# Feed-forward matmuls of a float32r transformer block: both activation parts as one 512-column moving operand, and the down projection after all gates and ups

## The chip, the cores and the metric

The kernel runs on one NeuronCore of a Trainium2 chip. The metric is device time in microseconds (us) of one execution; the table below gives the median of several. TensorE (PE) does the matrix products, with weight loads shown apart as PEld; VectorE (DVE), ScalarE (ACT) and GpSimd (POOL) do the element-wise work; SyncE (SP) issues nearly all DMA transfers.

## The reference, cut to what matters

Two transformer blocks act on 256 tokens of 1024 features. Between attention, a state-space mixer and a memory attention there are four feed-forward layers, all of the same form, with 2816 hidden features:

```
hn = rmsnorm(x, gain)
x = x + f * (silu(hn @ w_gate) * (hn @ w_up)) @ w_down      # f = 1 (twice), then 0.5 (twice)
```

`w_gate` and `w_up` are 1024 x 2816 and `w_down` is 2816 x 1024, all in float32, and all weights come from HBM once.

## The kernel before, in words

**Layout.** Activations lie with features on the partitions: `xt` is [128, 8 blocks of 128 features, 256 tokens]. Each operand is kept in two parts, a rounded one (high, names ending in h, or `whi`) and what is left of it (low, names ending in l, or `wlo`), both in the type float32r. `mm3` (lines 306 to 308) makes a product of high by high, high by low and low by high, so three matmuls of 256 columns for each k-tile of 128 rows and each block of 128 output rows. The weights are the stationary operand, and each matmul has its own weight load.

**Weights.** The weights are cut on the host into slabs of [128, 2048] (1 MB). `_make` loads a slab into `raw` (two buffers, SP's queue), and cuts each half of 1024 columns: ACT rounds it to `whi` (L279), DVE subtracts to make `wlo` (L281). `whi` and `wlo` have five buffers of half a slab each, and a slab is made two slabs ahead of its use. One slab feeds 48 matmuls.

**A feed-forward layer** (`ffn`) walks over 11 chunks of 256 hidden features. A chunk has a gate slab, an up slab and a down slab. `gemm_feat` fills one PSUM bank with two blocks of 256 tokens; it uses the first half of the slab (k-tiles 0 to 3) for both blocks, then the second half. DVE scales the gate bank (L522), ACT applies Silu (L523), POOL scales once more (L524); DVE multiplies the up bank by it (L528), ACT rounds (L531) and DVE subtracts (L532), which gives the down projection's operand `hh`, `hl`. The down projection of the chunk before follows each chunk: `gemm_out` adds its two k-tiles to four PSUM banks (`acc`) that live through the whole layer. At the end `add` adds the four banks to `xt`, one after the other (L510, or L512 with the factor 0.5).

**Order.** A scheduler orders the instructions of each engine when the kernel is built, by priority and by when it takes operands to be ready; each engine then runs its list in that order. `norm` makes the next layer's operand out of `xt` (ACT L438, DVE L439, squares on ACT and POOL) at high priority; the factor of each token (`rb`) is multiplied in after the matmuls, so that the matmuls don't wait for it.

Of the kernel before, what the change touches and what calls it, by code (L numbers as in the profile page):

```python
# [52 lines left out]
def weight_plan():  # L53
# [14 lines left out]
    def ffn(kind, layer):  # L68
        for c in range(11):
            feat(f"{kind}_gate", layer, c * 256, 256)  # L70
            feat(f"{kind}_up", layer, c * 256, 256)
            if c >= 1:
                out(f"{kind}_down", layer, 2 * (c - 1), 2)
        out(f"{kind}_down", layer, 20, 2)
# [7 lines left out]
    # layer 0  # L82
# [11 lines left out]
    # layer 1  # L94
# [8 lines left out]
    # second block  # L103
# [50 lines left out]
def pack_weights(w):  # L154
# [24 lines left out]
    for s, (name, layer, kind, k0, n0) in enumerate(weight_plan()):  # L179
        nk, n = {"f": (8, 256), "t": (4, 512), "o": (2, 1024)}[kind]  # L180
        out[s].reshape(P, nk, n)[:] = rows(mats[(name, layer)], k0, nk, n0, n)
# [3 lines left out]
def pack_params(w):  # L185
# [16 lines left out]
    def states(a):  # L202
        # [32 groups, 64 states, ...] -> [(half, state), 16 groups of a half, ...]
# [19 lines left out]
# ---------------------------------------------------------------- the program  # L223
class Kernel:
# [15 lines left out]
    # -- tiles  # L240
# [15 lines left out]
    # -- weights: a slab comes in float32 and is cut into two parts of 12 bits each  # L256
    def _make(self, upto, first=None):
        nc = self.nc
        while self.made <= min(upto, len(self.plan) - 1):
# [4 lines left out]
            else:  # L264
                # the first slab comes in parts, among those of its operand
# [44 lines left out]
    def operand(self, pool=None, tag="a"):  # L310
        """Four k-tiles of a transposed activation for all tokens, in two parts."""
# [1222 lines left out]
```

## Time and profile before

| | |
|---|---|
| time, median of 3 runs | 1269.5 us (1267.67 to 1269.79) |
| profiled execution: span | 1268.1 us |
| PE busy / PEld busy | 1232.9 us (97%) / 1184.7 us (93%) |
| DVE busy / ACT busy / POOL busy | 797.9 us (63%) / 619.3 us (49%) / 211.6 us (17%) |
| matmuls | 9798 |
| HBM read | 205.57 MB, 164 GB/s over the span |

The span is that of the one profiled execution, and every duration below is from it; it lies 1.4 us under the median of the runs. A busy time is a union: matmuls overlap one another in the trace (a 256-column matmul lasts 0.28 us, the next one starts before it ends), so a matmul's price is the distance between two starts.

### The profile page before, as it was taken

The page shows a single profiled execution, that of the slowest core. Times are in us where ns is not written, and L with a number is a line of the kernel's source. Part 1 is how long each engine was busy: PE and PEld are TensorE (multiplying, and loading weights), DVE is VectorE, ACT ScalarE, POOL GpSimd, SP SyncE. Part 2 cuts the span into 40 slices and gives each one's busy share as a digit, 9 for nine tenths or more (in the row PEclk, how much of TensorE's full clock was granted, in tenths as well). Part 3 has the DMA queues.
Part 4 walks back from the last instruction along what each step waited for, and adds up shares of the span by engine and source line. Part 5 has one row for each costly group of instructions (what it writes and reads, how often), then busy time and mean ns, then how long its engine had stood idle before and what let it go on. Part 6 is the DMA issues. An engine that isn't in the chain of part 4 may idle for free.

```text
span 1268.1 us, 23060 instructions
## 1 busy us (share of the span) xinstructions
PE 1232.9 (97%) x9798; PEld 1184.7 (93%) x9798; DVE 797.9 (63%) x967; ACT 619.3 (49%) x875; POOL 211.6 (17%) x177
## 2 busy tenths in 40 slices
PE   5898999999999999999999999999999999999997
PEld 5777999999999789999999999998889999999997
DVE  8988575555576548655557555557766666655553
ACT  6553564344457656444445444446664544544343
POOL 7674030000020003000002000002301102100001
PEclk9987999999999999999999999999999999999998
DMA  6552345445553225545545545546532434545441
GB/s 208 165 169 70 125 177 199 170 168 195 199 173 133 100 91 201 178 169 195 200 169 186 181 170 197 195 172 208 201 132 101 163 107 160 204 168 198 168 170 63
DMA packets 36791, 209.12 MB, mean 165 GB/s; under 512 B 3920, under 2 KB 9808, under 8 KB 12752
## 3 DMA queue, kind: packets, MB, share of 16 engines
q1 hardware_dynamic: 35824, 205.48, 46.2%
q8 instruction: 77, 1.26, 0.4%
q0 software_dynamic: 576, 1.64, 0.4%
q10 hardware_dynamic: 288, 0.52, 0.1%
q14 instruction: 26, 0.21, 0.0%
HBM read 205.57 MB, written 2.06 MB: 164 GB/s over the span
## 4 chain that ended last, share of the span: by engine, by line
PE 88%; DVE 7%; DMA 2%; issue 1%; ACT 1%; POOL 0%; DVEq 0%; ACTq 0%; POOLq 0%
PE mm L306 15%; PE mm L307 15%; PE mm L308 15%; PE acc L308 11%; PE acc L306 11%; PE acc L307 11%; DVE wlo L281 2%; DMA raw<-in_wts 1%; PE tr L378 1%; PE acc L1166 1%; DVE al L439 1%; PE acc L601 1%; PE tr L396 1%; PE mm L567 1%; PE acc L1193 1%
## 5 line engine op out<-in xcount | busy, mean ns | idle before, releaser
L281 DVE TENSOR_TENSOR wlo<-raw,whi 128x1024 fp32r<-128x1024 f32 (+1 forms) x378 | 468.1, 1249 | 309.9 <-ACT whi L279 305.1
L279 ACT CAST whi<-raw 128x1024 fp32r<-128x1024 f32 (+1 forms) x378 | 388.4, 1042 | 421.8 <-PE acc L307 174.3
L306 PE MATMUL mm<-ah,whi 128*128 128x256 f32 x1504 | 425.8, 284 | 6.9 <-ACT whi L279 6.5
L308 PE MATMUL mm<-ah,wlo 128*128 128x256 f32 x1504 | 426.6, 284 | 0.8 <-DVE wlo L281 0.7
L307 PE MATMUL mm<-al,whi 128*128 128x256 f32 x1504 | 426.7, 284 | 0.0
L306 PEld LDWEIGHTS mm<-ah,whi 128*128 128x128 f32 x1504 | 289.0, 193 | 8.1 <-ACT whi L279 6.8
L308 PEld LDWEIGHTS mm<-ah,wlo 128*128 128x128 f32 x1504 | 289.4, 193 | 1.7 <-DVE wlo L281 1.5
L307 PEld LDWEIGHTS mm<-al,whi 128*128 128x128 f32 x1504 | 289.5, 193 | 0.6
L307 PE MATMUL acc<-hl,whi 128*128 128x256 f32 x704 | 199.3, 283 | 0.2 <-DVE hl L532 0.2
L308 PE MATMUL acc<-hh,wlo 128*128 128x256 f32 x704 | 199.1, 283 | 0.0
L306 PE MATMUL acc<-hh,whi 128*128 128x256 f32 x704 | 198.8, 283 | 0.0
L524 POOL TENSOR_TENSOR sg<-sg,rb 128x512 f32<-128x512 f32 x44 | 59.8, 1358 | 599.0 <-ACT sg L523 599.0
L307 PEld LDWEIGHTS acc<-hl,whi 128*128 128x128 f32 x704 | 135.1, 192 | 0.5 <-DVE hl L532 0.4
L308 PEld LDWEIGHTS acc<-hh,wlo 128*128 128x128 f32 x704 | 135.2, 192 | 0.0
L306 PEld LDWEIGHTS acc<-hh,whi 128*128 128x128 f32 x704 | 134.9, 192 | 0.2 <-ACT hh L531 0.2
L307 PE MATMUL acc<-al,whi 128*128 128x256 f32 x368 | 104.2, 285 | 0.0
L308 PE MATMUL acc<-ah,wlo 128*128 128x256 f32 x368 | 103.3, 284 | 0.0
L306 PE MATMUL acc<-ah,whi 128*128 128x256 f32 x368 | 102.2, 285 | 0.0
L448 POOL TENSOR_TENSOR ssq<-ssq,sq 128x512 f32<-128x512 f32 x26 | 42.4, 1629 | 275.0 <-issue 158.4
L523 ACT ACTIVATE sg<-sg 128x512 f32<-128x512 f32 x44 | 27.8, 631 | 97.8 <-DVE sg L522 97.8
L307 PEld LDWEIGHTS acc<-al,whi 128*128 128x128 f32 x368 | 70.6, 192 | 0.2
L308 PEld LDWEIGHTS acc<-ah,wlo 128*128 128x128 f32 x368 | 70.2, 192 | 0.2
(378 smaller groups left out, 1563.6 us busy)
## 6 DMA issues: line engine op xcount, KB each, us to landing
raw<-in_wts SPq DMA_DIRECT2D x187, 1024.0 KB, 4.9
raw<-in_mem SPq DMA_DIRECT2D x4, 512.0 KB, 4.7
eb<-lag SPq DMA_DIRECT2D x4, 512.0 KB, 4.7
x<-in_x SPq DMA_DIRECT2D x4, 256.0 KB, 5.1
raw<-in_wts SPq DMA_DIRECT2D x4, 256.0 KB, 5.3
sprm<-in_prm SPq DMA_DIRECT2D x1, 512.0 KB, 9.0
ud<-s SPq DMA_DIRECT2D x1, 512.0 KB, 2.6
uu<-ud SPq DMA_DIRECT2D x8, 64.0 KB, 4.4
```

The source lines that it names most:

```text
L279: nc.scalar.copy(hi[:, c:c + n], src)
L281: nc.vector.tensor_tensor(lo[:, c:c + n], src, hi[:, c:c + n].bitcast(F32), ALU.subtract)
L306: mm(out, a[0], b[0], start=start, stop=False, skip_group_check=True)
L307: mm(out, a[0], b[1], start=False, stop=False, skip_group_check=True)
L308: mm(out, a[1], b[0], start=False, stop=stop, skip_group_check=True)
L378: self.nc.tensor.transpose(out, in_, self.ident[:k, :k])
L396: nc.tensor.matmul(ps[:, t:t + 1], sq[:, t * P:(t + 1) * P], self.ones[:, 0:1], start=(i == 0 and t == 0), stop=(i == len(sqs) - 1), skip_ ...
L439: lo = nc.vector.scalar_tensor_tensor(lo, x[:, b, :], g, hi.bitcast(F32), ALU.mult, ALU.subtract).ins
L448: nc.gpsimd.tensor_tensor(ssq, ssq, q, ALU.add)
L523: nc.scalar.activation(sg, sg, AF.Silu)
L524: nc.gpsimd.tensor_tensor(sg, sg, rb2, ALU.mult)
L567: nc.tensor.matmul(scv[:, i, :], qt[r, qb, t * P:(t + 1) * P], kt[r, kblock(qb), 0:keys], start=False, stop=(i == per - 1))
```

## The change

In the feed-forward layers the high and the low part of an activation lie in one tile, one behind the other. A product with a high weight part streams both parts in one matmul of 512 columns, into a bank whose first 256 columns are the sum for the high part and whose last 256 are that for the low part; a low weight part streams the high activations alone (256 columns, added to the first 256). So a block of 128 output rows takes a whole bank, and evacuating it adds the two halves: ACT copies the second half out, DVE adds the first (in `half`), and the gate's scaling reads SBUF. All 11 chunks' gates and ups come first, and their outputs stay in 11 tiles `h0` to `h10`. Then the down projection goes by output blocks: 22 k-tiles into one bank, and two DVE operations that add its halves to `xt`. The down slabs hold 16 tiles of 128 x 128 in that order. Operands elsewhere use the same joined tile but are multiplied by `mm3` as before. An unused option of `norm` and the comments are gone.

```diff
 def ffn(kind, layer):                      # in weight_plan
         for c in range(11):
             feat(f"{kind}_gate", layer, c * 256, 256)
             feat(f"{kind}_up", layer, c * 256, 256)
-            if c >= 1:
-                out(f"{kind}_down", layer, 2 * (c - 1), 2)
-        out(f"{kind}_down", layer, 20, 2)
+        for c in range(11):
+            plan.append((f"{kind}_down", layer, "d", c * 16, 0))
...
+class Parts(tuple):
+    def __new__(cls, x):
+        self = super().__new__(cls, (x[:, 0], x[:, 1]))
+        self.both = x
+        return self
...
     def operand(self, pool=None, tag="a"):
         if pool is not None:
-            return tuple(self.t(pool, [P, 4, 256], tag + x, F32R) for x in "hl")
-        return tuple(self.t(self.ap4, [P, 4, 256], "a" + x, F32R, bufs=self.A_BUFS) for x in "hl")
+            x = self.t(pool, [P, 2, 4, 256], tag, F32R)
+        else:
+            x = self.t(self.ap4, [P, 2, 4, 256], "a", F32R, bufs=self.A_BUFS)
+        return Parts(x)
...
+    def mm2(self, out, w, x, first, last):
+        mm = self.nc.tensor.matmul
+        mm(out[:, 0, :], w[1], x[:, 0], start=first, stop=False, skip_group_check=True)
+        mm(out, w[0], x, start=False, stop=last, skip_group_check=True)
...
     def ffn(self, kind, layer, gain, factor):
...
+        def half(ps, dst):
+            v = ps.rearrange("p (i t) -> p i t", i=2)
+            y = self.t(fp, [P, 256], "half", bufs=4)
+            nc.scalar.copy(y, v[:, 1])
+            nc.vector.tensor_tensor(dst, v[:, 0], y, ALU.add)
+
+        def products(name, c, tag, evac):
+            w = self.slab(f"{kind}_{name}", layer, "f", 0, c * 256)
+            for b in range(2):
+                ps = self.ps(tag)
+                out = ps.rearrange("p (i t) -> p i t", i=2)
+                for k in range(8):
+                    self.mm2(out, w(k * 256 + b * P, P), ops[k // 4].both[:, :, k % 4, :], k == 0, k == 7)
+                evac(b, ps)
 
         for c in range(11):
             sg = self.t(fp, [P, 2, 256], "sg", bufs=2)
...
+            h = self.t(fp, [P, 2, 256], "h", bufs=2)
+            x = self.t(fp, [P, 2, 2, 256], f"h{c}", F32R)
+            hs.append(x)
+            products("gate", c, "acc", lambda b, ps, sg=sg: half(ps, sg[:, b]))
+            nc.vector.tensor_tensor(sg, sg, rb2, ALU.mult)
+            nc.scalar.activation(sg, sg, AF.Silu)
+            nc.gpsimd.tensor_tensor(sg, sg, rb2, ALU.mult)
+            products("up", c, "mm", lambda b, ps, h=h: half(ps, h[:, b]))
+            nc.vector.tensor_tensor(h, h, sg, ALU.mult)
+            nc.scalar.copy(x[:, 0], h)
+            nc.vector.tensor_tensor(x[:, 1], h, x[:, 0].bitcast(F32), ALU.subtract)
+        n = 0
+        for o in range(8):
+            ps = self.ps("acc")
+            out = ps.rearrange("p (i t) -> p i t", i=2)
+            for k in range(22):
+                if n % 16 == 0:
+                    w = self.slab(f"{kind}_down", layer, "d", n, 0, ahead=LASTF if n == 160 else None)
+                self.mm2(out, w(n % 16 * P, P), hs[k // 2][:, :, k % 2, :], k == 0, k == 21)
+                n += 1
+            with self.tc.high_priority(offset=self.HASTE):
+                y = self.t(fp, [P, 256], "y", bufs=2)
+                x = self.xt[:, o, :]
+                nc.vector.scalar_tensor_tensor(y, out[:, 0], factor, x, ALU.mult, ALU.add)
+                nc.vector.scalar_tensor_tensor(x, out[:, 1], factor, y, ALU.mult, ALU.add)
```

The first place is TensorE's list where the last feed-forward layer begins. Before, `mm` 11361 is the gate's bank and `mm` 11423 the up's; `ah`, `al` are the operand's parts.

```order
L306 MATMUL mm_11361<-ah_11307,whi_11185 128x256
L306 MATMUL mm_11423<-ah_11307,whi_11243 128x256
L307 MATMUL mm_11361<-al_11308,whi_11185 128x256
L308 MATMUL mm_11361<-ah_11307,wlo_11186 128x256
L306 MATMUL mm_11361<-ah_11307,whi_11185 128x256
L307 MATMUL mm_11423<-al_11308,whi_11243 128x256
L308 MATMUL mm_11423<-ah_11307,wlo_11244 128x256
```

In the changed kernel `a` is the joined tile; the two `acc` banks are the gate's two blocks, the two `mm` banks the up's.

```order
L366 MATMUL acc_10250<-a_10196,wlo_10075 128x256
L366 MATMUL mm_10303<-a_10196,wlo_10133 128x256
L366 MATMUL mm_10323<-a_10196,wlo_10133 128x256
L366 MATMUL acc_10270<-a_10196,wlo_10075 128x256
L367 MATMUL acc_10250<-a_10196,whi_10074 128x512
L366 MATMUL acc_10250<-a_10196,wlo_10075 128x256
L367 MATMUL acc_10270<-a_10196,whi_10074 128x512
L366 MATMUL acc_10270<-a_10196,wlo_10075 128x256
```

Three matmuls of 256 columns have become one of 256 and one of 512, a low weight part now comes first, and four blocks of gate and up are taken in turn as the k-tiles come, as before.

The second place is VectorE's list over one chunk in the middle of the gates and ups of the last layer. Before, with a down slab in the chunk:

```order
L522 TENSOR_TENSOR sg_12598<-mm_12609,rb_11348 128x512
L281 TENSOR_TENSOR wlo_12664<-raw_12661,whi_12663 128x1024
L281 TENSOR_TENSOR wlo_12668<-raw_12661,whi_12667 128x1024
L528 TENSOR_TENSOR h_12720<-mm_12671,sg_12598 128x512
L281 TENSOR_TENSOR wlo_12729<-raw_12726,whi_12728 128x1024
L532 TENSOR_TENSOR hl_12723<-h_12720,hh_12722 128x512
L281 TENSOR_TENSOR wlo_12733<-raw_12726,whi_12732 128x1024
L281 TENSOR_TENSOR wlo_12788<-raw_12785,whi_12787 128x1024
L281 TENSOR_TENSOR wlo_12792<-raw_12785,whi_12791 128x1024
```

In the changed kernel (L526 is the add of a bank's two halves, L544 the gate's scaling, L548 the product, L550 the low part):

```order
L526 TENSOR_TENSOR sg_11000<-acc_11013,half_11030 128x256
L550 TENSOR_TENSOR h_1863_10893<-h_10892,h_1863_10893 128x512
L295 TENSOR_TENSOR wlo_11010<-raw_11003,whi_11009 128x1024
L526 TENSOR_TENSOR sg_11000<-acc_11033,half_11050 128x256
L295 TENSOR_TENSOR wlo_11059<-raw_11056,whi_11058 128x1024
L544 TENSOR_TENSOR sg_11000<-sg_11000,rb_10235 128x512
L526 TENSOR_TENSOR h_11001<-mm_11066,half_11083 128x256
L295 TENSOR_TENSOR wlo_11063<-raw_11056,whi_11062 128x1024
L526 TENSOR_TENSOR h_11001<-mm_11086,half_11103 128x256
L295 TENSOR_TENSOR wlo_11115<-raw_11112,whi_11114 128x1024
L548 TENSOR_TENSOR h_11001<-h_11001,sg_11000 128x512
```

A chunk has two slabs instead of three, so four cuts instead of six, and four adds are new among them.

The third place is ScalarE's list where the last chunk's hidden features are rounded. Before, `hh` is that of the last chunk, and `ssq` is the final norm's square:

```order
L523 ACTIVATE sg_13156<-sg_13156 128x512
L279 CAST whi_13221<-raw_13219 128x1024
L279 CAST whi_13225<-raw_13219 128x1024
L531 CAST hh_13280<-h_13278 128x512
L1443 ACTIVATE ssq_13388<-x_78 128x512
```

In the changed kernel `raw` 11383 is the second down slab, `raw` 11437 the third, and L525 is the copy of a bank's second half:

```order
L545 ACTIVATE sg_11327<-sg_11327 128x512
L293 CAST whi_11389<-raw_11383 128x1024
L525 COPY half_11430<-mm_11413 128x256
L293 CAST whi_11439<-raw_11437 128x1024
L293 CAST whi_11443<-raw_11437 128x1024
L549 CAST h_1947_11329<-h_11328 128x512
L293 CAST whi_11481<-raw_11479 128x1024
```

The last chunk's rounding (L549) now stands behind both cuts of the third down slab.

## Rows read from the trace of the kernel before

**Rows 1.** The page: busy times, chain that ended last.
```profile
PE 1232.9 (97%) x9798; PEld 1184.7 (93%) x9798; DVE 797.9 (63%) x967; ACT 619.3 (49%) x875; POOL 211.6 (17%) x177
PE 88%; DVE 7%; DMA 2%; issue 1%; ACT 1%; POOL 0%; DVEq 0%; ACTq 0%; POOLq 0%
```

**Rows 2.** Windows: us; PE, PEld, DVE, ACT, POOL busy; granted clock; DMA share; GB/s.
```profile
520.00:537.28 17.28, 17.28 (x146) 17.28 (x145) 9.50 (x10) 7.25 (x8) 1.30 (x1) 1.00 0.52 184
700.00:860.00 160.00, 160.00 (x1336) 160.00 (x1335) 88.66 (x85) 66.88 (x74) 11.72 (x9) 1.00 0.52 185
```

**Rows 3.** Timeline of TensorE, feed-forward: start us, us, instruction; 20 starts from first to last.
```profile
330.00 0.28 PE L306 MATMUL acc<-hh,whi 128*128 128x256 f32 x1
...
332.40 0.28 PE L308 MATMUL acc<-hh,wlo 128*128 128x256 f32 x1
```

**Rows 4.** Timeline of TensorE, 512-column matmuls of the mixer; 18 starts from first to last.
```profile
869.82 0.39 PE L307 MATMUL acc<-wlo,ah 128*128 128x512 f32 x1
...
873.90 0.39 PE L307 MATMUL acc<-wlo,ah 128*128 128x512 f32 x1
```

**Rows 5.** Timeline of TensorE, 512 columns between 256 columns, in layer 1's attention.
```profile
412.80 0.40 PE L1193 MATMUL acc<-sph,trih 128*128 128x512 f32 x1
413.03 0.28 PE L308 MATMUL mm<-ah,wlo 128*128 128x256 f32 x1
413.15 0.28 PE L306 MATMUL mm<-ah,whi 128*128 128x256 f32 x1
...
413.39 0.40 PE L1193 MATMUL acc<-sph,trih 128*128 128x512 f32 x1
413.63 0.28 PE L308 MATMUL mm<-ah,wlo 128*128 128x256 f32 x1
```

**Rows 6.** Timeline of TensorE, a 512-column moving operand read as two rows of 256.
```profile
922.57 0.40 PE L563 MATMUL mm<-dilh,identr 128*128 128x512 f32 x1
922.80 0.40 PE L563 MATMUL mm<-dill,identr 128*128 128x512 f32 x1
```

**Rows 7.** Groups by line, 700 to 860 us: xcount, busy us, mean ns, idle before.
```profile
L281 DVE TENSOR_TENSOR wlo<-raw,whi 128x1024 fp32r<-128x1024 f32 x56 | 70.1, 1265 | 57.9 <-ACT whi L279 57.6
L279 ACT CAST whi<-raw 128x1024 fp32r<-128x1024 f32 x55 | 56.7, 1047 | 67.4 <-PE acc L307 35.8 <-PE mm L307 31.6
L524 POOL TENSOR_TENSOR sg<-sg,rb 128x512 f32<-128x512 f32 x9 | 11.7, 1302 | 142.0 <-ACT sg L523 142.0
L532 DVE TENSOR_TENSOR hl<-h,hh 128x512 fp32r<-128x512 f32 x10 | 6.8, 683 | 0.0
L528 DVE TENSOR_TENSOR h<-mm,sg 128x512 f32<-128x512 f32 x9 | 6.2, 691 | 6.3 <-PE mm L308 6.3
L531 ACT CAST hh<-h 128x512 fp32r<-128x512 f32 x10 | 6.2, 615 | 0.2 <-DVE h L528 0.2
L523 ACT ACTIVATE sg<-sg 128x512 f32<-128x512 f32 x9 | 5.7, 632 | 24.2 <-DVE sg L522 24.2
```

**Rows 8.** Timeline, single operations on 256 columns: ACT out of PSUM, DVE on SBUF.
```profile
1261.23 0.37 ACT L408 COPY rb<-tr 128x256 f32<-128x256 f32 x1 [0.79 <-PE tr L406]
483.27 0.87 DVE L439 SCALAR_TENSOR_TENSOR al<-x,prm,ah 128x256 fp32r<-128x256 f32 x2
```

**Rows 9.** Timeline, second feed-forward layer: first matmuls, last piece of its operand.
```profile
484.75 0.40 PE L306 MATMUL mm<-ah,whi 128*128 128x256 f32 x2
490.61 2.40 DVE L439 SCALAR_TENSOR_TENSOR al<-x,prm,ah 128x256 fp32r<-128x256 f32 x2
```

**Rows 10.** Timeline, end of the last feed-forward layer: last add, square, mean.
```profile
1255.84 0.69 DVE L512 SCALAR_TENSOR_TENSOR x<-acc,x 128x512 f32<-128x512 f32 x1 [0.74 <-PE acc L308]
1256.62 0.63 ACT L1443 ACTIVATE sq<-x 128x512 f32<-128x512 f32 x1 [0.86 <-DVE x L512]
1258.63 0.16 DVE L400 TENSOR_SCALAR rs<-tr 128x2 f32<-128x2 f32 x1 [2.10 <-PE tr L396]
```

**Rows 11.** Waits of SP's queue, 520 to 860 us: total us, times, longest.
```profile
SPq L263 <- DVE wlo L281: 289.9, 59, 7.9
```

More of the change, by code (lines that the diff above doesn't have):

```diff
@@ L179, in pack_weights @@
     for s, (name, layer, kind, k0, n0) in enumerate(weight_plan()):
+        if kind == "d":
+            for j in range(16):
+                o, k = divmod(k0 + j, DFF // P)
+                out[s][:, j * P:(j + 1) * P] = mats[(name, layer)][k * P:(k + 1) * P, o * P:(o + 1) * P]
+            continue
         nk, n = {"f": (8, 256), "t": (4, 512), "o": (2, 1024)}[kind]
@@ L411, in inv_rms, with norm, _norm @@
         return rb, [r[:, t:t + 1] for t in range(nt)]
-    def norm(self, x, gain, tag="rb", make=True, haste=True, pool=None, whole=False, soon=False):
+    def norm(self, x, gain, tag="rb", make=True, haste=True, pool=None, soon=False):
         if not haste:
-            return self._norm(x, gain, tag, make, pool, whole, soon)
+            return self._norm(x, gain, tag, make, pool, soon)
         with self.tc.high_priority(offset=self.HASTE):
-            return self._norm(x, gain, tag, make, pool, whole, soon)
-    def _norm(self, x, gain, tag, make, pool, whole, soon):
+            return self._norm(x, gain, tag, make, pool, soon)
+    def _norm(self, x, gain, tag, make, pool, soon):
         nc = self.nc
         ops = None
-        if whole:
-            ops = [(self.t(self.ap4, [P, 4, 256], x, bufs=self.A_BUFS),) for x in ("ah", "al")]
-        elif make:
+        if make:
             ops = [self.operand(pool, f"m{i}") for i in range(2)]
@@ L457, in _norm @@
             sqs = [ssq[:, :256]]
-        if x is self.xt and make and not whole and self.at:
+        if x is self.xt and make and self.at:
             pin, self.pin = self.pin, lo if PINN else self.pin
@@ L503, in ffn @@
         rb2 = rb.unsqueeze(1).to_broadcast([P, 2, 256])
-        acc = None
-        hts = {}
-        def add(pr, ps):
-            x = self.xt[:, 2 * pr:2 * pr + 2, :]
-            if factor == 1.0:
-                nc.vector.tensor_tensor(x, ps, x, ALU.add)
-            else:
-                nc.vector.scalar_tensor_tensor(x, ps, factor, x, ALU.mult, ALU.add)
-        def down(c, done=None):
-            w = self.slab(f"{kind}_down", layer, "o", 2 * c, 0, ahead=LASTF if c == 10 else None)
-            self.gemm_out(acc, w, [hts.pop(c)], (0, 1), c == 0, c == 10, done)
+        hs = []
@@ L518, in ffn @@
         for c in range(11):
             sg = self.t(fp, [P, 2, 256], "sg", bufs=2)
-            def gate(_, ps):
-                nc.vector.tensor_tensor(sg, ps, rb2, ALU.mult)
-                nc.scalar.activation(sg, sg, AF.Silu)
-                nc.gpsimd.tensor_tensor(sg, sg, rb2, ALU.mult)
-            def up(_, ps):
-                h = self.t(fp, [P, 2, 256], "h", bufs=2)
-                nc.vector.tensor_tensor(h, ps, sg, ALU.mult)
-                hi = self.t(fp, [P, 2, 256], "hh", F32R, bufs=2)
-                lo = self.t(fp, [P, 2, 256], "hl", F32R, bufs=2)
-                nc.scalar.copy(hi, h)
-                nc.vector.tensor_tensor(lo, h, hi.bitcast(F32), ALU.subtract)
-                hts[c] = (hi, lo)
@@ L535, in ffn @@
-            tag = "acc" if c == 1 else "mm"
-            self.gemm_feat(ops, f"{kind}_gate", layer, c * 256, 256, gate, tag)
-            self.gemm_feat(ops, f"{kind}_up", layer, c * 256, 256, up, tag)
-            if c == 1:
-                acc = [self.ps("acc") for _ in range(4)]
-            if c >= 1:
-                down(c - 1)
-        down(10, add)
+            h = self.t(fp, [P, 2, 256], "h", bufs=2)
+            x = self.t(fp, [P, 2, 2, 256], f"h{c}", F32R)
+            hs.append(x)
@@ L946, in ssm_in @@
         gts = []
-        for q in range(4):
-            gts.append(self.t(self.ap4, [P, 2, 4, 8, 16], "ah" if q % 2 == 0 else "al", F32, bufs=self.A_BUFS))
+        for q in range(2):
+            x = self.t(self.ap4, [P, 2, 2, 4, 8, 16], "a", F32, bufs=self.A_BUFS)
+            gts += [x[:, 0], x[:, 1]]
         def outs(q):
```

6 lines of the change are left out of this document (removed).

## Prediction

> **What bounds the kernel now.** I read the page first. TensorE is busy 97% of the span, and 88% of the chain that ended last is TensorE's [rows 1]; no other engine passes 63%. Then the windows: inside a feed-forward layer TensorE is busy for all of a 160 us stretch with the clock at 1.00, that is at the upper of its two levels, 2.4 GHz, while DVE is busy 55% and ACT 42% of it [rows 2]. So within these layers a change pays exactly what it takes off TensorE's stream, as long as no other engine becomes later than the stream. The third view is the timeline, because busy times of overlapping matmuls say nothing of their price: 20 starts of 256-column matmuls take 2.40 us, 120.0 ns each [rows 3]; 1336 of them in 160 us is the same number [rows 2]. A layer has 11 x 3 slabs x 48 = 1584 such matmuls, 190.1 us; the four layers take 760 us of the 1268.
>
> **What the change removes from TensorE.** For each k-tile and each block of 128 output rows, three matmuls of 256 columns (360 ns) become one of 256 and one of 512. The columns are the same, 768; a start is saved. There are 1584 / 3 = 528 such triples in a layer and 2112 in all. What the saved start is worth depends on the price of a 512-column float32r matmul:
>
> - In a long stream of them, 18 starts take 4.08 us, 226.7 ns each [rows 4]. The columns that a 512 has over a 256 cost 106.7 ns, which is 256 columns at 2.4 GHz; so both widths carry the same 13.3 ns on top of their columns, and that is what goes with the third matmul. A pair would take 120 + 226.7 = 346.7 ns: 13.3 ns saved, 2112 times, 28.1 us.
> - Where a 512 stands between 256s, which is the form that the change makes, it takes 0.23 us, and the 256 behind it 0.12 [rows 5]; in the same short stretch one takes 0.24. A moving operand read as two rows of 256, as the joined tile is, also takes 0.23 [rows 6]. With 230 ns the pair takes 350 and 10 ns are saved: 21.1 us. With 0.24 nothing is saved.
>
> The long stream settles at its price after some starts, and the new stream is as long and as regular, so I don't take the single places alone; they are nearest in form, so I don't take the stream alone either. I take the middle of 346.7 and 350, 348.4 ns: 11.6 ns x 2112 = 24.5 us. Both ends stay in the range, and 0.24 is a rival. The weight loads fall from three to two. PEld is busy through the whole stretch too [rows 2], so they could be what sets the 120 ns; but a 512 gives the next load nearly twice the time and carries the same 13.3 ns [rows 4], so I count nothing for the load that goes, and keep it as a rival.
>
> The Trainium skill ("TensorE: Matmul & The Clock Gate", Part 1 and the section on the back-to-back issue gap) says that a warm matmul starts N / 2.4 GHz plus about 2.5 ns after the one before. By that a triple would cost 3 x 2.5 ns over its columns and the pair 2 x 2.5, and the change would give 2112 x 2.5 ns = 5.3 us. The rows here have 13.3 ns in place of 2.5, at both widths, and the sum goes by the rows.
>
> **What it adds, and what hides it.** Each bank's two halves must be added: four ACT copies and four DVE adds of 256 columns for each chunk. A chunk of gate and up now takes 32 pairs, 11.15 us. ACT in it: four cuts at 1.047, Silu 0.632, the rounding 0.615 [rows 7] and four copies at 0.37 [rows 8] make 6.9 us. DVE: four cuts at 1.265, three operations on 512 columns at about 0.69 [rows 7], and four adds. An add of 256 columns out of PSUM has no row; one on SBUF costs 0.44 (two in 0.87) [rows 8], one on 512 columns out of PSUM 0.69 [rows 7]. With 0.44, nearer in size, DVE needs 8.9 us, with 0.69 9.9. Both are under 11.15, so the adds lie beside the stream. If that cover went, each us above 11.15 would cost 44 us (44 chunks). The down slabs need less: two cuts and about one add of `xt` for 5.6 us.
>
> *Weights.* A gate or up slab is now read through for its first block, then for its second, so its first half comes free at three quarters of the slab instead of at half. With five half-slab buffers the cut of the second half of the slab after next then starts at three quarters of this slab and is needed at a quarter of that one: 1.5 slabs, 8.4 us, for 2.3 us of work [rows 7]. SP's queue today waits for DVE to free `raw`, up to 7.9 us at a time [rows 11], so transfers have room; the same bytes move.
>
> *Queued behind such a wait.* The copies of a bank's half stand behind these cuts on ACT's list. A gate bank has four buffers, and an up bank's next use is 8.4 us after its end, so a cut that waits for the current slab to be used up delays nothing that TensorE needs.
>
> *Start of the down projection.* ACT rounds the last chunk behind the cuts of the third down slab (the third place shown above), and the second of these cuts waits until half of the first down slab is used: 8 pairs, 2.8 us. Then cut, DVE's subtraction of it, and the low part of the hidden features: 2.8 + 1.05 + 1.27 + 0.68 = 5.8 us [rows 7]. TensorE needs it at the 21st of 22 k-tiles, 7.0 us. The slack is 1.2 us, so I count nothing; without it this costs under 2 us a layer.
>
> *Start of a layer.* Today the last piece of the operand is ready 8.3 us after the first matmul (490.61 + 2.40 less 484.75) [rows 9], and nothing waits long because gate and up are worked on together. In the changed list the last k-tile's low part is needed after some 38 pairs' worth of work less what is put off: by the list's columns at these prices, 9.7 us. Slack 1.4 us; if it goes, some 1 to 2 us in each of four layers.
>
> *End of a layer.* The blocks of `xt` now become ready one by one, 7.7 us apart, and only the last is late. Behind the last matmul of all stand two dependent operations of 0.44 us [rows 8] instead of one add of 0.69 [rows 10], then the same square and the same sum: +0.2 us. After the other three layers the next product starts with earlier k-tiles, and only the last one or two of eight wait for this.
>
> *Elsewhere.* Operands in joined tiles give the scheduler slightly other orders in the first layer's mixer; I count zero, plus or minus 3 us.
>
> **Sum.** Span 1268.1 - 24.5 + 0.2 = 1243.8 us. The median of the runs lies 1.4 us above the span, so 1245.2. With the ends of the pair's price: 1241.6 to 1248.6.
>
> **The rivals.**
> - *Waits at the seams.* The slacks of 1.2 and 1.4 us are small, and lists are in order. For it: DVE's pieces stretch to 1.2 us when POOL adds squares beside them (2.40 for two, against 0.87) [rows 8, 9]. Against it: today's layers start with the same work. Eight seams at 1 us: 1253.
> - *A 512 costs more when it alternates.* At 235 ns the pair takes 355, and 10.6 us are left: 1259. From 240 ns on nothing is saved (1270), and each further ns costs 2.1 us. For it: the one row of 0.24 [rows 5]; against it: its neighbours and the stream [rows 4, 5, 6].
> - *DVE becomes the bound of gates and ups*, the case on the slow side as a mechanism of its own. Place: the 44 chunks. It begins at 11.15 us of DVE for each chunk and undoes the whole gain at 11.7 (44 x 0.56 = 24.5). I have 8.9 to 9.9; POOL works 1.3 us in a chunk [rows 2], and if DVE did nothing in that time it would be 11.2 at the worst. At 12 us: 1283.
> - *The third matmul gives back little*: the 13.3 ns belong to the pair of weights and not to the start, so that only some 2.5 ns go: 5.3 us, 1264. The 512's own 13.3 [rows 4] speaks against it. The rule of the Trainium skill named above would put the time here.
> - *The 256 behind a 512 is cheaper* because its weights had twice the time to load. At 110 ns the pair takes 337 with the stream's 226.7: 48 us, 1221. The row behind a 512 has 0.12 [rows 5].
> - That the change does nothing can't be: the list shows the pairs.
>
> **Chances.** Likeliest case 0.68; seams 0.13; alternating price between 351 and 360 ns 0.06; little given back 0.03; pair or DVE on the slow side 0.05; cheaper than 1241 0.05. The predicted time is that of the likeliest, 1245. The range from 1236 to 1257 leaves out the slow side, the cases near 1260 and the far end of the fast side. About 0.2% (2.5 us) is what a measurement of this kernel can tell from no change: the shown runs spread over 2.1 us. Faster 0.93, same 0.02, slower 0.05.
>
> **What would show it.** In the changed profile: starts that alternate 0.12 and 0.23 us in the feed-forward layers (right), or 0.24 and more (wrong price); the stretch of a layer down from 190 to about 184 us; no idle of TensorE put down to ACT's copies, DVE's adds or the cuts; DVE's busy share in gates and ups near 80%, in the down part near 60%; matmuls down by 2112 to some 7690. Idle in front of the first matmul on a half-ready operand, or before the last chunk's k-tiles of the first output block, would speak for the seams. The prediction is wrong if the pair does not take 346 to 351 ns, or if TensorE waits by chunks.

## The result, and the profile after

The changed kernel takes 1246.6 us (median of 4 runs, 1243.8 to 1252.7) against 1268.9 us of the kernel before; the ratio is 0.9834, with a 95% interval of 0.9807 to 0.9861. The profiled execution has a span of 1242.1 us, 26.0 us less than before. 1245 was forecast for the median and 1243.8 for the span.

The page, busy times and chain, which answer to [rows 1]:

```profile
PE 1211.7 (98%) x7686; PEld 1072.7 (86%) x7686; DVE 868.8 (70%) x1191; ACT 676.6 (54%) x1052; POOL 211.2 (17%) x177
PE 92%; DVE 5%; DMA 1%; issue 1%; ACT 1%; POOL 0%; DVEq 0%; ACTq 0%
```

TensorE still ends the chain, with a larger share than before, and 7686 matmuls are left of 9798. The windows of the second layer, once in gates and ups and once in the down projection (columns as in [rows 2]):

```profile
500.00:590.00 90.00, 90.00 (x521) 79.38 (x520) 70.25 (x96) 52.79 (x85) 11.63 (x9) 1.00 0.53 187
605.00:660.00 55.00, 55.00 (x314) 47.75 (x313) 37.34 (x45) 26.83 (x33) 2.94 (x3) 1.00 0.55 194
```

TensorE is busy for every microsecond of both, at the upper level of its clock. DVE is busy 78% of the first (80% was forecast) and 68% of the second (60%). Now the timeline of TensorE (start, us, instruction): two pairs of gates and ups, and the same place 30 pairs later; then two starts of the down projection, also 30 pairs apart.

```profile
530.13 0.28 PE L366 MATMUL mm<-a,wlo 128*128 128x256 f32 x1
530.24 0.39 PE L367 MATMUL mm<-a,whi 128*128 128x512 f32 x1
530.47 0.28 PE L366 MATMUL mm<-a,wlo 128*128 128x256 f32 x1
530.59 0.39 PE L367 MATMUL mm<-a,whi 128*128 128x512 f32 x1
...
540.53 0.28 PE L366 MATMUL acc<-a,wlo 128*128 128x256 f32 x1
...
640.21 0.28 PE L366 MATMUL acc<-h,wlo 128*128 128x256 f32 x1
640.33 0.40 PE L367 MATMUL acc<-h,whi 128*128 128x512 f32 x1
640.57 0.28 PE L366 MATMUL acc<-h,wlo 128*128 128x256 f32 x1
...
650.81 0.28 PE L366 MATMUL acc<-h,wlo 128*128 128x256 f32 x1
```

Starts alternate 0.12 and 0.23 us, as forecast. But the two stretches differ: 30 pairs take 10.40 us in gates and ups, 346.7 ns each, and 10.60 us in the down projection, 353.3 ns each. Neither is the 348.4 of the prediction. Over all pairs of the four layers the distance behind a 256-column matmul averages 117.2 ns and that behind a 512-column one 232.2, 349.4 in sum.

The two layers in the middle follow one another, so they give a clean length. They begin at 484.75 before [rows 9] and 478.81 after, and the next product begins here, before:

```profile
867.08 0.40 PE L306 MATMUL acc<-whi,ah 128*128 128x512 f32 x1
```

and here, after (the first matmul of the layers and the first one behind them):

```profile
478.81 0.28 PE L366 MATMUL acc<-a,wlo 128*128 128x256 f32 x1
...
849.80 0.39 PE L320 MATMUL acc<-whi,a 128*128 128x512 f32 x1
```

That is 382.3 us before and 371.0 after. Read the same way, all four layers take 765.3 us before and 741.2 after (185.1, 185.1, 185.9 and 185.1): 24.1 us of the 26.0. The groups of DVE and ACT in gates and ups (500 to 590 us; columns as in [rows 7]):

```profile
L295 DVE TENSOR_TENSOR wlo<-raw,whi 128x1024 fp32r<-128x1024 f32 x32 | 40.8, 1277 | 16.8 <-ACT whi L293 16.8
L293 ACT CAST whi<-raw 128x1024 fp32r<-128x1024 f32 x32 | 33.5, 1047 | 8.6 <-DMA raw<-in_wts 8.3
L546 POOL TENSOR_TENSOR sg<-sg,rb 128x512 f32<-128x512 f32 x9 | 11.6, 1296 | 78.4 <-ACT sg L545 78.4
L526 DVE TENSOR_TENSOR h<-mm,half 128x256 f32<-128x256 f32 x16 | 6.6, 413 | 0.0
L544 DVE TENSOR_TENSOR sg<-sg,rb 128x512 f32<-128x512 f32 x9 | 6.1, 684 | 0.0
L525 ACT COPY half<-acc 128x256 f32<-128x256 f32 x16 | 5.8, 364 | 0.0
```

The new add of 256 columns out of PSUM, which had no row before, takes 0.41 us and the copy 0.36. A chunk costs DVE 4 x 1.277 + 4 x 0.413 + 3 x 0.684 = 8.8 us beside 11.1 us of TensorE. The end, as [rows 10] had it:

```profile
1230.35 0.42 DVE L565 SCALAR_TENSOR_TENSOR y<-acc,x 128x256 f32<-128x256 f32 x1 [6.89 <-PE acc L367]
1230.81 0.42 DVE L566 SCALAR_TENSOR_TENSOR x<-acc,y 128x256 f32<-128x256 f32 x1
1231.33 0.63 ACT L1468 ACTIVATE sq<-x 128x512 f32<-128x512 f32 x1 [13.53 <-DVE x L566]
```

From the first operation on the last bank to the square: 0.98 us, 0.78 before.

### The profile page after: what moved, and what is told of

Its sections match the earlier page's. It is cut to its first block, busy times and chain, and to the rows that moved or that the text cites. A ratio compares the mean times of both kernels' runs of the same rounds, so it can differ in the third digit from the quotient of the medians.

```text
span 1242.1 us, 19044 instructions
## 1 busy us (share of the span) xinstructions
PE 1211.7 (98%) x7686; PEld 1072.7 (86%) x7686; DVE 868.8 (70%) x1191; ACT 676.6 (54%) x1052; POOL 211.2 (17%) x177
## 4 chain that ended last, share of the span: by engine, by line
PE 92%; DVE 5%; DMA 1%; issue 1%; ACT 1%; POOL 0%; DVEq 0%; ACTq 0%
PE acc L367 26%; PE acc L366 13%; PE mm L367 13%; PE mm L366 7%; PE mm L320 4%; PE mm L322 4%; PE mm L321 4%; PE acc L322 4%; PE acc L321 4%; PE acc L320 4%; PE mm L591 1%; PE tr L401 1%; PE acc L1191 1%; DVE wlo L295 1%; PE acc L625 1%; DVE a L454 1%
## 5 line engine op out<-in xcount | busy, mean ns | idle before, releaser
L367 PE MATMUL acc<-h,whi 128*128 128x512 f32 x704 | 247.8, 397 | 0.0
L367 PE MATMUL mm<-a,whi 128*128 128x512 f32 x704 | 247.0, 392 | 0.0
L367 PE MATMUL acc<-a,whi 128*128 128x512 f32 x704 | 246.0, 392 | 0.0
L366 PE MATMUL acc<-h,wlo 128*128 128x256 f32 x704 | 196.9, 281 | 0.0
L366 PE MATMUL mm<-a,wlo 128*128 128x256 f32 x704 | 196.6, 281 | 0.0
L366 PE MATMUL acc<-a,wlo 128*128 128x256 f32 x704 | 196.3, 280 | 0.0
L367 PEld LDWEIGHTS acc<-h,whi 128*128 128x128 f32 x704 | 131.9, 188 | 32.0
L367 PEld LDWEIGHTS mm<-a,whi 128*128 128x128 f32 x704 | 131.5, 187 | 28.5
L367 PEld LDWEIGHTS acc<-a,whi 128*128 128x128 f32 x704 | 130.9, 187 | 28.2
L366 PEld LDWEIGHTS acc<-a,wlo 128*128 128x128 f32 x704 | 133.0, 189 | 1.0
L366 PEld LDWEIGHTS acc<-h,wlo 128*128 128x128 f32 x704 | 132.9, 189 | 0.3
L366 PEld LDWEIGHTS mm<-a,wlo 128*128 128x128 f32 x704 | 132.6, 189 | 0.2
L321 PE MATMUL acc<-a,whi 128*128 128x256 f32 x240 | 67.4, 284 | 0.0
L322 PE MATMUL acc<-a,wlo 128*128 128x256 f32 x240 | 67.1, 285 | 0.0
L322 PE MATMUL mm<-a,wlo 128*128 128x256 f32 x224 | 66.1, 296 | 0.8 <-DVE wlo L295 0.7
L320 PE MATMUL acc<-a,whi 128*128 128x256 f32 x240 | 66.0, 286 | 0.0
```

The source lines that it names most:

```text
L320: mm(out, a[0], b[0], start=start, stop=False, skip_group_check=True)
L321: mm(out, a[0], b[1], start=False, stop=False, skip_group_check=True)
L322: mm(out, a[1], b[0], start=False, stop=stop, skip_group_check=True)
L366: mm(out[:, 0, :], w[1], x[:, 0], start=first, stop=False, skip_group_check=True)
L367: mm(out, w[0], x, start=False, stop=last, skip_group_check=True)
```

## The experiments

### Is it the width? One matmul of 512 cut back into two

```diff
-        mm(out, w[0], x, start=False, stop=last, skip_group_check=True)
+        mm(out[:, 0, :], w[0], x[:, 0], start=False, stop=last, skip_group_check=True)
+        mm(out[:, 1, :], w[0], x[:, 1], start=False, stop=last, skip_group_check=True)
```

> The changed kernel, but the 512-column matmul is cut into two of 256 with the same weights; order, evacuation and slabs stay. Theory (the gain is the third start): three starts of 120 ns in place of 346.7 ns (gates and ups) and 353.3 ns (down), so each layer longer by 352 x 13.3 + 176 x 6.7 ns = 5.9 us, 191.0 us instead of 185.1, and the span about 1242 + 23.5 = 1265.6 us, within 0.3% of the kernel before. Rival (order, evacuation or slabs give the gain): the layers stay at 185 us and the span at about 1242. Half-way (1254) if both have a part.

Measured: 1268.0 us, ratio to the kernel before 0.9997 (0.998 to 1.0014). Its timeline in gates and ups has three equal starts again:

```profile
562.40 0.28 PE L366 MATMUL acc<-a,wlo 128*128 128x256 f32 x1
562.52 0.28 PE L367 MATMUL acc<-a,whi 128*128 128x256 f32 x1
562.64 0.28 PE L368 MATMUL acc<-a,whi 128*128 128x256 f32 x1
562.76 0.28 PE L366 MATMUL acc<-a,wlo 128*128 128x256 f32 x1
```

360 ns for the three, and layers of 191.2 us on average, as before the change (191.3). The order, the slabs and the evacuation are those of the changed kernel, so in the layers none of them gives anything that shows beside the 24 us: the gain is the start that the wider matmul saves, together with the weight load that goes with it. Those two are not told apart here, because the cut kernel has 9798 weight loads for its 9798 matmuls, one for each start.

### Why the down pair costs 353 ns: three layouts that are not the reason

Three kernels, one edit each: the moving operand as one row of 512 columns; its two rows 1024 columns apart, as in gates; the weights of successive pairs 256 columns apart, as in gates:

```diff
-            x = self.t(fp, [P, 2, 2, 256], f"h{c}", F32R)
-            hs.append(x)
+            y = self.t(fp, [P, 2, 2, 256], f"h{c}", F32R)
+            x = y.rearrange("p b i t -> p i b t")
+            hs.append(y)
...
-                self.mm2(out, w(n % 16 * P, P), hs[k // 2][:, :, k % 2, :], k == 0, k == 21)
+                self.mm2(out, w(n % 16 * P, P), hs[k // 2][:, k % 2, :, :], k == 0, k == 21)
```

```diff
-            x = self.t(fp, [P, 2, 2, 256], f"h{c}", F32R)
+            if c % 2 == 0:
+                pair = self.t(fp, [P, 2, 4, 256], f"h{c}", F32R)
+            x = pair[:, :, c % 2 * 2:c % 2 * 2 + 2, :]
```

```diff
-                out[s][:, j * P:(j + 1) * P] = mats[(name, layer)][k * P:(k + 1) * P, o * P:(o + 1) * P]
+                e = place(j) * P
+                out[s][:, e:e + P] = mats[(name, layer)][k * P:(k + 1) * P, o * P:(o + 1) * P]
...
+def place(j):
+    return j // 8 * 8 + j % 4 * 2 + j % 8 // 4
...
-                self.mm2(out, w(n % 16 * P, P), hs[k // 2][:, :, k % 2, :], k == 0, k == 21)
+                self.mm2(out, w(place(n % 16) * P, P), hs[k // 2][:, :, k % 2, :], k == 0, k == 21)
```

> The changed kernel, with the two parts of a k-tile of the hidden features one directly behind the other, so that the down projection's 512 columns are read as one row of 512 and not as two rows of 256 that lie 512 columns apart. Theory (what makes the down pair dearer than that of gates and ups, 353.3 against 346.7 ns, is the distance of its two rows): the down pair falls to 346.7 ns, a layer's 176 pairs to 61.0 us from 62.2, the span by 4 x 1.2 = 4.7 us to about 1237.5, 0.4% less. Rival (weights' places, or what other engines do meanwhile): the pair stays at 353 ns and the span at 1242.

> The changed kernel, with the hidden features of two chunks in one tile, so that the two rows of the down projection's 512-column operand lie 1024 columns apart, as those of gates and ups do, not 512. Theory (the distance of the rows makes the down pair dearer): 346.7 ns in place of 353.3, the span about 4.7 us less, 1237.5. Rival (weights' places, or what other engines do): 353 ns, 1242.

> The changed kernel, with the 128-column tiles of a down slab in another order, so that the weights of successive pairs lie 256 columns apart, as in gate and up slabs, and not 128; the moving operand is as it was. Theory of the rows' distance: nothing changes, the down pair takes 353 ns and the span is 1242. Rival (the places of the weights make the down pair dearer): 346.7 ns, and the span about 4.7 us less, 1237.5.

Measured: 1245.4, 1245.9 and 1247.5 us, ratios 0.9813, 0.9814 and 0.9822 with intervals some 0.002 to either side, not to be told from the changed kernel. Thirty pairs of the down projection of the first of them:

```profile
640.06 0.28 PE L366 MATMUL acc<-h,wlo 128*128 128x256 f32 x1
...
650.66 0.28 PE L366 MATMUL acc<-h,wlo 128*128 128x256 f32 x1
```

10.60 us here and in the two others. Both theories that I had named, the distance of the two rows and the places of the weights, fell.

### The reason: one break in the alternation

Pair by pair, the changed kernel's down projection begins at 346.7 ns and turns to 353.3 after some 30 of its 176 pairs. There the scheduler has put off the last chunk's k-tiles, presumably because it takes them to be ready late. TensorE's list at that place (`h` 2890 is the last chunk; `acc` 2997 and 3065 are the first two output blocks):

```order
L366 MATMUL acc_3065<-h_320_1909,wlo_2951 128x256
L367 MATMUL acc_3065<-h_320_1909,whi_2950 128x512
L366 MATMUL acc_2997<-h_509_2890,wlo_2947 128x256
L366 MATMUL acc_3065<-h_320_1909,wlo_2951 128x256
L367 MATMUL acc_3065<-h_320_1909,whi_2950 128x512
...
L367 MATMUL acc_2997<-h_509_2890,whi_2946 128x512
L367 MATMUL acc_3065<-h_362_2127,whi_2950 128x512
L366 MATMUL acc_3065<-h_362_2127,wlo_2951 128x256
```

Two matmuls of low weight parts (L366, called lows below) follow each other, and ten matmuls later two of high parts (L367, highs). Two kernels test this from both sides. The first gives the slabs an order in which nothing need be put off:

```diff
+DOWN = [(o, k) for o in range(8) for k in range(22)]
+DOWN = DOWN[:20] + DOWN[22:22 + 14] + DOWN[20:22] + DOWN[22 + 14:]
...
-        for o in range(8):
-            ps = self.ps("acc")
-            out = ps.rearrange("p (i t) -> p i t", i=2)
-            for k in range(22):
...
+        for n, (o, k) in enumerate(DOWN):
...
+            if k == 0:
+                outs[o] = self.ps("acc").rearrange("p (i t) -> p i t", i=2)
```

> The changed kernel, with the last chunk's two k-tiles of the first output block put 14 pairs later in the slabs' order, so that they are ready when they come, and TensorE's list holds low, high, low, high through the whole down projection; in the changed kernel two lows follow each other at one place there and two highs ten matmuls later, and from there on the pair takes 353.3 ns and not 346.7. Theory (that break of the alternation sets the dearer rhythm, which then holds): the down pair stays at 346.7 ns to the layer's end, a layer falls from 185.1 to about 184.1 us (150 pairs x 6.7 ns), the span by 4 us to 1238. Rival (something else in the down projection makes its pairs dearer after a while): 353 ns from the same place on, 1242.

The second breaks the alternation where there was no break. For four k-tiles of one block, the low of a k-tile goes ahead of the high of the k-tile before it:

```diff
+                    wk, x = w(k * 256 + b * P, P), ops[k // 4].both[:, :, k % 4, :]
+                    if c != 5 or name != "gate" or b == 0 or k in (0, 1, 6, 7):
+                        self.mm2(out, wk, x, k == 0, k == 7)
+                        continue
...
+                    mm(out[:, 0, :], wk[1], x[:, 0], start=False, stop=False, skip_group_check=True)
+                    if k > 2:
+                        mm(out, late[0], late[1], start=False, stop=False, skip_group_check=True)
+                    late = wk[0], x
+                    if k == 5:
+                        mm(out, late[0], late[1], start=False, stop=False, skip_group_check=True)
```

> The changed kernel, with the alternation broken once in each layer in the middle of the gates (chunk 6 of 11, second block): two lows, then high, low, high, low, then two highs. The same matmuls, none more or less. Theory (a break of the alternation sets a dearer rhythm, which holds until TensorE stands still): from there to the start of the down projection, about 5.4 chunks or 172 pairs, the pair takes 353.3 in place of 346.7 ns, a layer gets 1.1 us longer, the span 4.6 us (1246.7). Rival (the rhythm belongs to the down projection): the pairs stay at 346.7 ns and the span at 1242.

Measured, first kernel: 1241.5 us, ratio 0.9788 (0.9764 to 0.9812). Thirty pairs of its down projection (L370 is the 256-column matmul):

```profile
639.76 0.28 PE L370 MATMUL acc<-h,wlo 128*128 128x256 f32 x1
...
650.16 0.28 PE L370 MATMUL acc<-h,wlo 128*128 128x256 f32 x1
```

10.40 us, 346.7 ns each, and its layers take 184.1, 184.1, 184.9 and 184.1 us, 1.0 less each, as the theory said. Second kernel: 1248.6 us, ratio 0.9834 (0.9811 to 0.9858). Thirty pairs of gates behind the new break, then thirty of the down projection:

```profile
560.36 0.28 PE L366 MATMUL acc<-a,wlo 128*128 128x256 f32 x1
...
570.96 0.28 PE L366 MATMUL acc<-a,wlo 128*128 128x256 f32 x1
...
640.03 0.28 PE L366 MATMUL acc<-h,wlo 128*128 128x256 f32 x1
...
650.43 0.28 PE L366 MATMUL acc<-h,wlo 128*128 128x256 f32 x1
```

Behind the break gates cost 10.60 us, the dear rhythm, so it is no property of the down projection. What I had not expected is the second half: at the scheduler's own break it went back, and the down projection took 10.40. So a break does not set the dear rhythm, it lets the stream change between two. In all twelve breaks of the changed kernel and of this one the stream turns at the two highs; the two lows ahead of them leave it as it is. That the down projection goes back is why the layers are only 0.4 us longer (185.5), and not 1.1. What decides inside TensorE which of the two a break leaves behind is open.

### How much cover DVE has

Three, or five, more DVE operations of 512 columns in each chunk but a layer's first (for the second kernel read `5` for `3`), and then the first of these without POOL's scaling (the last line belongs to that third kernel alone):

```diff
+            for _ in range(3 if c else 0):
+                nc.vector.tensor_tensor(self.t(fp, [P, 2, 256], "junk"), hs[c - 1][:, 0].bitcast(F32), rb2, ALU.mult)
...
-            nc.gpsimd.tensor_tensor(sg, sg, rb2, ALU.mult)
```

> The changed kernel with three more DVE operations of 512 columns (0.68 us each) in each of the chunks 2 to 11 of gates and ups; nothing uses what they write. DVE's work for a chunk goes from 8.8 to 10.9 us, beside 11.1 us of TensorE. Theory of the prediction (DVE is hidden up to TensorE's time for a chunk): no change, span 1242 within 2 us. Rival (with lists in order, DVE must have far more room than its sum says): TensorE waits by chunks, some 0.5 us in each of 40, the span 1260 or more.

> The changed kernel with five more DVE operations of 512 columns in each of the chunks 2 to 11; nothing uses what they write. DVE's work for a chunk goes from 8.8 to 12.2 us. Theory of the prediction (DVE becomes the bound at TensorE's 11.1 us for a chunk): each of 40 chunks 1.1 us longer, the span about 45 us more, 1287, slower than the kernel before. Rival (part of the work can wait for the down projection, where DVE has room): less than half of it, under 1264.

> The kernel with three more DVE operations in a chunk, less POOL's scaling after Silu (left out, so the second factor of each token is missing from the product). DVE's list has the same order in a chunk. Theory (the waits of some 0.5 us by chunks come from the 2.3 us that a cut takes while POOL works, in place of 1.2): no cut over 1.5 us, no such waits, the layers at 185 to 186 us and the span 1242 to 1244. Rival (DVE's list is late by its sum, 10.9 us for a chunk, whatever POOL does): the waits stay and the span is about 1253.

Measured: with three, 1258.2 us, ratio 0.9921 (0.9895 to 0.9948), about 12 us lost to the changed kernel; with five, 1247.4, ratio 0.9826 (0.981 to 0.9843), and with three and without POOL's operation, 1247.3, ratio 0.9826 (0.9808 to 0.9845), neither to be told from it. Three operations cost where the prediction's theory had nothing, though less than the rival's 1260; five cost almost nothing, as their rival had it (under 1264), and against the theory's 1287. The timeline of the kernel with three, at one of its waits, on DVE, POOL and PE:

```profile
564.96 2.33 DVE L295 TENSOR_TENSOR wlo<-raw,whi 128x1024 fp32r<-128x1024 f32 x1
...
567.55 1.21 DVE L295 TENSOR_TENSOR wlo<-raw,whi 128x1024 fp32r<-128x1024 f32 x1
...
564.92 1.29 POOL L546 TENSOR_TENSOR sg<-sg,rb 128x512 f32<-128x512 f32 x1 [10.41 <-ACT sg L545]
...
566.61 0.39 PE L367 MATMUL mm<-a,whi 128*128 128x512 f32 x1
567.34 0.39 PE L366 MATMUL mm<-a,wlo 128*128 128x256 f32 x1 [0.35 <-DVE wlo L295]
```

The cut that starts with POOL's operation takes 2.33 us, the next one 1.21: 1.1 us more, and TensorE, which wants that cut, waits. But the cuts are not TensorE's longest waits. Its waits over the second and third layer (total us, times, longest), and the long cut, the product and the rounding ahead of the first:

```profile
PE acc L366 <- ACT h L551: 1.2, 1, 1.2
PE mm L366 <- DVE wlo L295: 0.6, 2, 0.3
```

```profile
611.36 2.33 DVE L295 TENSOR_TENSOR wlo<-raw,whi 128x1024 fp32r<-128x1024 f32 x1
...
615.08 0.68 DVE L550 TENSOR_TENSOR h<-h,sg 128x512 f32<-128x512 f32 x1
...
615.79 0.62 ACT L551 CAST h<-h 128x512 fp32r<-128x512 f32 x1 [2.41 <-DVE h L550]
```

A long cut beside POOL's operation delays the last chunk's product and so its rounding (`h` L551), and the down projection waits for that. It does so in the first, second and fourth layer, 1.4, 1.2 and 1.5 us. The four layers are 10 us longer than in the changed kernel, 4.7 of it in the down projections. This is the slack of 1.2 us that the prediction had at the start of the down projection.

Without POOL's operation DVE has the same work for a chunk, its cuts take 1.22 us on average and the layers 185.1, 185.1, 185.9 and 185.1 us, with no such wait. So POOL's operation makes the waits. By way of long cuts is what the timelines show; leaving it out also makes the product ready sooner, and that part was not tested by itself. The windows of 500 to 590 us bear on why five did less harm than three; first the kernel with three, then in a fence of its own the one with five:

```profile
500.00:590.00 90.00, 89.64 (x513) 78.26 (x513) 84.37 (x120) 51.92 (x85) 13.80 (x9) 1.00 0.50 176
```

```profile
500.00:590.00 90.00, 90.00 (x521) 79.46 (x520) 87.30 (x131) 52.44 (x85) 19.28 (x9) 1.00 0.52 180
...
L548 DVE TENSOR_TENSOR junk<-h,rb 128x512 f32<-128x512 f32 x33 | 24.8, 750 | 0.0
```

With five, DVE is busy 97% of the stretch and TensorE waits for nothing. About four of the five extra operations run there (33 in 8.1 chunks), and the list puts others off into the down projection, as the rival had it. And POOL's nine operations take 19.3 us in place of 11.6: here it is POOL that is held up. TensorE waits once in the four layers of this kernel, 1.5 us at the start of the second down projection, again for the last chunk's rounding. So a cover is not used up by DVE's sum alone: what cost was a cut that fell together with POOL's operation, in front of something that TensorE needed soon. How soon matters: the third layer of the kernel with three has such long cuts too and takes 185.7 us without a wait.

### Less work for TensorE: does DVE's sum become the bound?

```diff
-        mm(out[:, 0, :], w[1], x[:, 0], start=first, stop=False, skip_group_check=True)
-        mm(out, w[0], x, start=False, stop=last, skip_group_check=True)
+        mm(out, w[0], x, start=first, stop=last, skip_group_check=True)
```

> The changed kernel without the products of the low weight parts (2112 matmuls of 256 columns left out; the weights are still cut in two), so that TensorE's stream in the feed-forward layers is 512-column matmuls alone: 32 x 226.7 ns = 7.25 us for a chunk. DVE still has 8.8 us of work for a chunk, and 1.3 us of POOL beside it. Theory (DVE bounds gates and ups where its sum is above TensorE's): a chunk takes 8.8 us, or 9.9 to 10.1 where POOL's operation stands beside a cut; 97 to 111 us for 11 chunks, 40 for the down part, a layer 138 to 152 us, the span 1050 to 1108. Rival (the sum of DVE's work doesn't bound, work can be put off): a layer of 121 us, the span about 985.

Measured, a single run: 1103.6 us, span 1101.9. The second layer's first matmul of the gates and first of the down projection:

```profile
445.62 0.63 PE L366 MATMUL acc<-a,whi 128*128 128x512 f32 x2
...
544.53 0.74 PE L366 MATMUL acc<-h,whi 128*128 128x512 f32 x2 [0.56 <-ACT whi L293]
```

98.9 us for 11 chunks, 9.0 each (8.9 to 9.3 in the four layers), where TensorE alone would need 7.25. That is near DVE's sum of 8.8, as the theory said, but it does not show that the sum is the bound. Inside gates and ups (first row), and in the down projection (second row), and what TensorE and ACT waited for in gates and ups:

```profile
452.00:544.00 92.00, 81.08 (x335) 62.38 (x333) 84.35 (x128) 63.68 (x106) 22.39 (x14) 0.96 0.62 221
545.00:591.00 46.00, 41.59 (x171) 30.83 (x170) 36.64 (x45) 26.34 (x34) 5.12 (x3) 1.00 0.70 245
```

```profile
PE acc L366 <- ACT whi L293: 8.7, 6, 6.2
ACT whi L293 <- DMA raw<-in_wts: 16.9, 12, 3.0
```

DVE is busy 92% of gates and ups, but TensorE waits there for ACT's rounding of weights, ACT for the transfer, and the transfer for DVE to free one of the two `raw` buffers. In the down projection DVE is busy 80%, and its 11 slabs take 46.4 to 47.5 us for the 40 expected: TensorE waits in the same way. A slab costs 4.2 to 4.3 us there, so two cost 8.4 to 8.6 without any work on gates and ups. The round of transfer, rounding and cut over two buffers thus gives almost the same time as DVE's sum, and this run can't tell them apart.

### The better order, beside the changed kernel on one chip

> The changed kernel again, beside the next one on the same chip. Both theories: 1243 to 1248 us, as it was.

> The kernel with the last chunk's two k-tiles of the first output block put 14 pairs later, again. If its four layers are shorter by 1.0 us each, as its trace showed, it should be 4 us under the changed kernel of the same chip, 1239 to 1244; if the difference of the two medians came from the first mixer's clock, the two are equal within 2 us.

Measured: 1244.7 us (1243.3 to 1247.3, 6 runs) and 1241.4 us (1240.0 to 1242.6, 5 runs), ratios 0.9799 (0.9774 to 0.9824) and 0.9771 (0.9747 to 0.9795). The intervals of the ratios overlap, because the runs of the kernel before spread; the runs of the two kernels themselves do not. In their profiles the four layers take 741.2 and 737.2 us, the 4.0 less that were expected. The order without a break is 3.3 us faster than the changed kernel, and the fastest that was found with all products in it.

## Why the prediction was right, by its own steps

- **Price of the pair.** Right as a mean, 349.4 ns for the forecast 348.4: 10.6 ns x 2112 = 22.4 us for 24.5. That the mean fell so near the middle of the two ends is luck: no long stretch has that price, and without the break the mean is 347.5. The working was not right in detail. It took one price between two ends, 346.7 and 350; in truth there are two rhythms, the stream's own price of 346.7, which the changed kernel has in gates and ups, and 353.3, beyond the upper end. The sentence that failed is that the new stream would be as regular as the long stream of 512s: one break in the order is enough. The sign that it named, 346 to 351 ns, holds for gates and ups and for the mean, and not for the pairs behind the break. What the layers gave on top, 24.1 - 22.4 = 1.7 us, is 2.5 us that the old layers' matmuls took over 120.0 ns each in short waits and irregular starts, less 0.8 us for eight other matmuls that now stand inside the third layer.
- **Little given back by the third matmul.** Refuted: cutting the 512 in two brought the layers from 185 back to 191 us. A 256-column start costs 13.3 ns over its columns, and the saved one gave between 6.7 and 13.3. By the Trainium skill ("TensorE: Matmul & The Clock Gate", Part 1) a warm matmul costs about 2.5 ns over its columns, from which the change would be worth an estimated 5.3 us; no run here agrees. Whether the 13.3 ns belong to the start or to its weight load, which the prediction kept as a rival, stays open: no run has a start without a load of its own. For the start speaks, as the prediction argued, that a 512 leaves its neighbour's load nearly twice the time and carries the same 13.3 ns.
- **Evacuation hidden.** Right: 8.8 us of DVE for a chunk where 8.9 was forecast, with an add of 0.41 us (0.44 taken), 6.9 of ACT, and no idle of TensorE in either window.
- **Weights, seams.** Right: the longest distance between two starts within a layer is 0.42 us, next to the two matmuls that spread the tokens' factor. No wait for the last chunk's low part, and none for the last piece of the operand. But the late last chunk was not free: the scheduler's answer to it is the break that makes some 150 of a layer's pairs dearer, 1.0 us a layer. I had asked only whether TensorE would wait.
- **End.** Forecast +0.2, measured +0.2 (0.98 for 0.78).
- **Elsewhere.** Forecast 0 plus or minus 3. The first layer begins 1.2 us later (165.58 for 164.41), the two stretches between layers are 0.4 and 2.4 us shorter, what follows the last layer 0.4: 1.9 us gained in all. Executions of one kernel differ by as much there: run again, the changed kernel began its first layer at 167.4 us. So this may well be chance. With the 1.7 us above, this made up for the 2.1 us that the pair gave less than forecast; the span is as near as it is (1242.1 for 1243.8) because these cancel in part.
- **DVE as the bound.** It did not happen, and its price was wrong in both directions. I had waits begin at 11.15 us of DVE in a chunk. They began at a sum of 10.9, where POOL's operation made cuts long, and at a busy share of 97% there was one, of 1.5 us, in four layers. That the sum is a bound at all is not shown by any run.

## What to carry to other kernels

Where a stream of matmuls is TensorE's whole time, count starts as well as columns: joining two parts of the moving operand under one weight load saved 13.3 ns each time while the stream kept its rhythm, and the evacuation cost nothing that showed, with DVE and ACT busy 78% and 59% of just that stretch. Read the price of such a stream over tens of pairs and in each phase: a single put-off pair changed it here for a hundred pairs and more, and giving the producer time by the order of the data was 1.0 us a layer cheaper than leaving it to the scheduler. Before trusting an engine's sum as cover, look at which of its operations stand beside POOL's, and how long before its use each ends.

## What the runs showed of the hardware that I had not expected

**Two rhythms.** The same pairs of a 256- and a 512-column matmul run at 346.7 ns or, in a cycle of three pairs with distances of 114, 232, 118, 241, 120 and 235 ns, at 353.3 ns. Each held for over a hundred pairs, and in these traces it changed only at a break in the alternation (at two highs, or where other matmuls stand in between) or when the stream stopped. The triples of 256 columns showed no second one: 120.0 ns in [rows 3] and over the 160 us of [rows 2].

**DVE and POOL exclude one another.** A cut of 1024 columns took 2.33 us beside POOL's 1.29 us and 1.21 alone; in the kernel with five more operations POOL's took 2.4 us and more instead. The Trainium skill ("Trainium Architecture — The Big Picture", "What this means for kernel authors") says that these two share a port pair of SBUF under an exclusive lock; the rows agree, since the two together last 2.4 us in either case where one behind the other would make 2.5. Which of the two has to wait was not settled: with three and with five more operations the cut's record can begin some 45 ns behind POOL's, and in the one the cut is long, in the other POOL's operation.

**The clock of the first mixer moves the whole time.** In the profiled executions of the changed kernel and its variants the first feed-forward layer begins at 163.4 to 172.3 us, although the work ahead of it is the same. From 80 to 120 us, first in the changed kernel and then in the one with weights 256 columns apart, whose work there is the same:

```profile
80.00:120.00 40.00, 35.66 (x278) 27.12 (x279) 30.25 (x49) 15.57 (x44) 28.30 (x22) 0.79 0.24 71
```

```profile
80.00:120.00 40.00, 37.47 (x261) 27.35 (x261) 25.32 (x42) 12.93 (x40) 26.80 (x21) 0.53 0.18 58
```

With a granted clock of 0.79 the first layer begins at 165.6 us, with 0.53 at 172.3, and with 0.53 in the kernel with the 512 cut in two also at 172.3. This alone is more than the order without a break gives, so a few microseconds had to be read from the layers in the trace and not from a span.
